# Two feed-forward passes: twelve of the 22 channel pairs made by seven 256-column block products each instead of eight, with the block adds on VectorE

## The chip, the core and the metric

The kernel runs on one core of one Trainium2 chip. A core has five engines that run their own instruction queues in order and meet at semaphores: TensorE (PE in the profile, with its weight loads as PEld), VectorE (DVE), ScalarE (ACT), GpSimd (POOL) and SyncE (SP), which here issues the DMAs. On-chip memory is SBUF, the matmuls write PSUM. The metric is the device time of one execution in microseconds; lower is better.

## The reference

The reference is a decoder trunk of two layers over 1024 positions of width 1024, float32. Each layer has a mixer and then a feed-forward pass, and each of the four sub-layers ends as x <- LayerNorm(alpha * x + f(x)). The change is in the feed-forward pass alone:

- up: u = x @ w_up, from 1024 to 5632 channels, in two halves of 2816;
- a causal depthwise convolution of width 3 over positions on all 5632 channels, plus a bias;
- gelu (tanh form) of the first half times the second half;
- down: from 2816 channels to 1024.

Products have to be of float32 accuracy.

## The kernel before, in words

**Tiles.** The 1024 positions are worked in two halves h of 512. A pass F(h, l) is the feed-forward pass of half h in layer l, so there are four: F00, F10, F01 and F11 (the program writes half and then layer). The input x of a pass lies transposed in SBUF, channels on partitions, as XTh and XTl: every float32 operand is split in a rounded part (h, sh, wh, ph) and a rest (l, sl, wl, pl), and `mm3` makes a product of three matmuls, h·l, l·h and h·h. A weight block of 128 by 1024 float32 (512 KB) comes by DMA into one of three `wraw` buffers; ACT copies it to `wh` in one instruction of 1024 columns, and POOL subtracts, two of 512 columns, to `wl` (`wload`).

**A pass.** `up(j)` makes channel pair j of 22: for each of two channel tiles, 8 blocks of K times three matmuls into one PSUM bank `pu` of 512 columns, so 48 matmuls of 128x512 a pair. Then the three taps of the convolution: one ACT instruction, two scalar_tensor_tensor (STT) on DVE, all of 512 columns; for h = 0 a copy of the last two columns for the other half (`halo`), for h = 1 two one-column ACT instructions with the correction `cor`. ACT makes the gelu of the first tile, POOL multiplies the two tiles, and ACT and POOL split the product into ph and pl. `down` takes the pairs in three groups (KG: 8, 8 and 6), in products of 512 columns into `pd` banks; DVE adds each bank to Z, the running sum of the sub-layer. F11 has its last group in `down_last`, which hands rows to the final norm.

**What sets the order.** The program text is written as generators, which `go(F, n)` runs for n steps and `mix(A, F, n)` interleaves; the scheduler under it then fixes an order for each engine. At the start of F00 the norm of the other half, `norm(1, g0)`, is mixed into its first steps; at the start of F11 the final norm of half 0 stands between its steps. PSUM has 2 banks for `pu`, 2 for the tag "c" and 4 for `pd`. The code around the change is printed here.

## Time and profile before

| what | value |
|---|---|
| median of 3 runs | 2339.61 us (2338.78 to 2342.55) |
| the profiled execution | 2340.53 us |
| its span, first to last instruction | 2338.8 us |
| PE busy | 2293.3 us, 98% |
| PEld, DVE, ACT, POOL busy | 82%, 50%, 43%, 60% |
| mean granted TensorE clock | 0.995 of full speed |
| F00's 22 pairs and their downs, about 568 to 910 us | PE busy 339.11 of 342.00 us |
| F11, about 1973 us to the end | PE busy 354.48 of 365.00 us |

The profiled execution is 1.7 us longer than its span, which lies outside the first and last instruction, and it is 0.9 us above the median of the runs. A busy PE is one whose pipeline holds some matmul; two of them overlap, so the time that a matmul costs is read from start to start, not from its duration.

### The profile page before, as it was taken

To read this page: it belongs to the slowest core of one execution; us is meant where nothing else is said; L and a number is where in the kernel's file an instruction comes from. 1 tells how busy PE (TensorE), PEld (TensorE's weight loads), DVE (VectorE), ACT (ScalarE), POOL (GpSimd) and SP (SyncE) were. 2 spreads that over 40 slices of the span, in tenths; PEclk is the share of its full clock that TensorE was granted. 3 is DMA by queue.
4 is the path that set the end of the run, shared out by engine and by line. 5 is a ranking of instruction groups with operands and counts; after the bars stand their busy time and mean duration, and the time that the engine had idled before them with its cause. 6 is when DMAs were issued, how large, how long until landed. Compare 5 with 4: busy or idle time off the path is not lost.

```text
span 2338.8 us, 30101 instructions
## 1 busy us (share of the span) xinstructions
PE 2293.3 (98%) x10959; PEld 1914.5 (82%) x10959; DVE 1176.0 (50%) x2176; ACT 1008.9 (43%) x1786; POOL 1391.8 (60%) x1313
## 2 busy tenths in 40 slices
PE   9999899999999999999999999999999999999998
PEld 7888789887888888788888887788888887888886
DVE  2532898746322223579972325589961446212214
ACT  4133998733433323434344552434243633534441
POOL 4442777556665656655566575655565666666672
PEclk9999999999999999999999999999999999999999
DMA  6153121352332333233323233223323233323340
GB/s 227 35 144 98 50 64 54 105 194 92 99 99 90 99 95 95 84 97 99 99 91 99 90 108 101 85 95 100 99 91 99 89 110 135 96 95 99 99 135 37
DMA packets 82988, 232.23 MB, mean 99 GB/s; under 512 B 10079, under 2 KB 24039, under 8 KB 82840
## 3 DMA queue, kind: packets, MB, share of 16 engines
q1 hardware_dynamic: 82840, 230.30, 31.2%
q8 instruction: 87, 1.43, 0.3%
q14 instruction: 61, 0.50, 0.1%
HBM read 213.44 MB, written 8.43 MB: 95 GB/s over the span
## 4 chain that ended last, share of the span: by engine, by line
PE 93%; DVE 3%; ACT 1%; issue 1%; POOL 1%; DMA 0%; SPq 0%; DVEq 0%; ACTq 0%
PE pu L77 13%; PE pu L79 13%; PE pu L78 13%; PE pd L77 9%; PE pd L78 9%; PE pd L79 9%; PE pt L563 2%; PE pca L79 1%; PE pcg L79 1%; PE pcg L77 1%; PE pca L77 1%; PE pcg L78 1%; PE pca L78 1%; PE O L571 1%; PE O L570 1%
## 5 line engine op out<-in xcount | busy, mean ns | idle before, releaser
L73 POOL TENSOR_TENSOR wl<-wraw,wh 128x512 fp32r<-128x512 f32 x680 | 889.1, 1330 | 704.7 <-ACT wh L70 693.7
L77 PE MATMUL pu<-XTl,wh 128*128 128x512 f32 x1440 | 564.7, 392 | 5.9 <-DVE acc L683 3.7
L79 PE MATMUL pu<-XTh,wh 128*128 128x512 f32 x1440 | 563.6, 391 | 0.0
L78 PE MATMUL pu<-XTh,wl 128*128 128x512 f32 x1440 | 563.0, 391 | 0.0
L70 ACT ACTIVATE wh<-wraw 128x1024 fp32r<-128x1024 f32 x340 | 359.6, 1058 | 414.3 <-PE pd L79 352.9
L682 DVE SCALAR_TENSOR_TENSOR acc<-pu,vec,acc 128x511 f32<-128x511 f32 x176 | 131.8, 749 | 513.0 <-ACT acc L680 264.6
L77 PEld LDWEIGHTS pu<-XTl,wh 128*128 128x128 f32 x1440 | 271.8, 189 | 62.8 <-issue 4.1
L758 DVE SCALAR_TENSOR_TENSOR cacc<-ht,vec,cacc 128x512 f32<-128x512 f32 x464 | 318.5, 751 | 5.5 <-ACT cacc L754 3.9
L678 ACT ACTIVATE acc<-pu,vec 128x510 f32<-128x510 f32 (+1 forms) x176 | 137.3, 780 | 424.0 <-PE pu L79 423.8
L79 PEld LDWEIGHTS pu<-XTh,wh 128*128 128x128 f32 x1440 | 271.5, 189 | 56.8
L78 PEld LDWEIGHTS pu<-XTh,wl 128*128 128x128 f32 x1440 | 271.7, 189 | 56.2
L77 PE MATMUL pd<-wl,ph 128*128 128x512 f32 x656 | 259.1, 396 | 0.0
L78 PE MATMUL pd<-wh,pl 128*128 128x512 f32 x656 | 258.8, 394 | 0.0
L79 PE MATMUL pd<-wh,ph 128*128 128x512 f32 x656 | 256.7, 395 | 0.0
L79 PEld LDWEIGHTS pd<-wh,ph 128*128 128x128 f32 x656 | 123.5, 188 | 29.0
L78 PEld LDWEIGHTS pd<-wh,pl 128*128 128x128 f32 x656 | 123.7, 189 | 28.6
L77 PEld LDWEIGHTS pd<-wl,ph 128*128 128x128 f32 x656 | 123.6, 188 | 28.4
L398 DVE TENSOR_TENSOR Z<-Z,pd 128x512 f32<-128x512 f32 x64 | 43.5, 683 | 180.1 <-PE pd L79 180.0
L683 DVE SCALAR_TENSOR_TENSOR acc<-pu,vec,acc 128x510 f32<-128x510 f32 x176 | 131.5, 747 | 4.7
L690 POOL TENSOR_TENSOR acc<-acc 128x512 f32<-128x512 f32 x88 | 113.7, 1292 | 25.0 <-DVE acc L683 17.6
L396 DVE SCALAR_TENSOR_TENSOR Z<-Z,pd 128x512 f32<-128x512 f32 x64 | 43.6, 682 | 156.6 <-PE pd L79 156.6
L540 POOL TENSOR_SCALAR P<-P,sm 128x64 f32<-128x64 f32 (+6 forms) x192 | 107.4, 583 | 21.9 <-DVE sm L534 12.8
(252 smaller groups left out, 3790.4 us busy)
## 6 DMA issues: line engine op xcount, KB each, us to landing
wraw<-wup SPq DMA_DIRECT2D x176, 512.0 KB, 3.5
wraw<-wdn SPq DMA_DIRECT2D x82, 512.0 KB, 3.5
wraw<-cwin SPq DMA_DIRECT2D x32, 512.0 KB, 3.5
wraw<-wout SPq DMA_DIRECT2D x16, 512.0 KB, 4.3
wraw<-cwout SPq DMA_DIRECT2D x16, 512.0 KB, 3.5
wraw<-wab SPq DMA_DIRECT2D x14, 512.0 KB, 3.9
gb<-lns SPq DMA_DIRECT2D x12, 512.0 KB, 4.2
B<-fd SPq DMA_DIRECT2D x8, 512.0 KB, 3.4
```

The lines of the kernel that those rows point to most:

```text
L70: nc.scalar.activation(wh[:, :n], raw[:, :n], AF.Copy)
L73: (leng or nc.gpsimd).tensor_tensor(wl[:, c], raw[:, c], wh[:, c].bitcast(F32), op=OP.subtract)
L77: nc.tensor.matmul(out_, ah, bl, start=first, stop=False)
L78: nc.tensor.matmul(out_, al, bh, start=False, stop=False)
L79: nc.tensor.matmul(out_, ah, bh, start=False, stop=last)
L540: nc.gpsimd.tensor_scalar(P[:, e, o:o + ln_], P[:, e, o:o + ln_], sm[:, e, i:i + 1], 0.0, op0=OP.mult, op1=OP.add)
L563: nc.tensor.transpose(pt[:, j, e * 128:(e + 1) * 128], P[:, e, o:o + kn], ident)
L678: nc.scalar.activation(a[:, 2 * h:], p[:, 2 * h:], AF.Identity, scale=cw[:, mt, 2:3], bias=col(cb, mt))
L682: nc.vector.scalar_tensor_tensor(a[:, 1:], p[:, :511], cw[:, mt, 1:2], a[:, 1:], op0=OP.mult, op1=OP.add)
L683: nc.vector.scalar_tensor_tensor(a[:, 2:], p[:, :510], cw[:, mt, 0:1], a[:, 2:], op0=OP.mult, op1=OP.add)
L690: nc.gpsimd.tensor_tensor(acc[0], acc[0], acc[1], op=OP.mult)
L758: nc.vector.scalar_tensor_tensor(c[0] if k else ht[:, :H], ht[:, k:k + H], dww[:, j, k:k + 1], c[0], op0=OP.mult, op1=OP.add)
```

## The change

It adds `QUICK = (4, 16)` and a flag `quick`, which F00 and F11 set. In such a pass the pairs 4 to 15 go through `up7` instead of `up`. `up7` sees the pair as a 2 by 2 by 2 block product (two channel tiles, two halves of K of 512, two halves of the positions of 256) and makes it of seven block products, in the Strassen-Winograd form. Each is 4 blocks of K times three matmuls of 128x256, so 84 matmuls of 256 columns a pair. That asks for:

- sums of weights: `prep(j)` makes s1 to s4 and the block w22' (the first operand of the last product) out of the two raw blocks `ra` and `rb` by 4 adds of 512 columns on DVE, and splits s1, s2 and s4 by ACT (sh) and DVE (sl); the four other blocks are split as before by ACT (wh) and POOL (wl);
- sums of x: `sums()`, run once a pass in six steps within the pairs 1 to 3, makes TA and TB, four sums with a split of each, on POOL, DVE and ACT;
- sums of products: a copy of 256 columns on ACT and 5 adds of 256 columns on DVE (`tt`, and back into PSUM `pa` and `pb`).

In all pairs of the two passes the product of the two halves and its rest `pl` move from POOL to DVE (`gated`). The downs of the first 16 pairs go in four groups of 4 pairs instead of two of 8, one unit of 24 matmuls beside each pair from 3 on, so a pass adds a bank to Z 32 times for the first 16 pairs where it was 16 times. TA and TB take the slots that the other half's XTh and XTl have, so `norm(1, g0)` comes after 32 steps of F00 instead of at its start, with its two rows of factors loaded again; in F11 one step instead of two goes beside each part of the final norm of half 0.

The diff, cut to its core (`taps3` is the old code of the taps, moved into a function; `mm3` gets a flag that changes no instruction):

```diff
+QUICK = (4, 16)
...
-    def ffn(h, l, tail=None):
+    def ffn(h, l, tail=None, quick=False):
...
+        def gated(j, acc):
+            eng = nc.vector if quick else nc.gpsimd
+            eng.tensor_tensor(acc[0], acc[0], acc[1], op=OP.mult)
+            hi = fp.tile([128, 512], F32R, name="ph", tag="p", bufs=18)
+            lo = fp.tile([128, 512], F32R, name="pl", tag="p", bufs=18)
+            split(hi, lo, acc[0], eng)
+            prod[j] = (hi, lo)
...
+        def sums():
+            ta, tb = A("xh", F32R, (128, 4, 4, 256), name="TA"), A("xl", F32R, (128, 4, 4, 256), name="TB")
+            X7["11"], X7["21"], X7["22"] = ((xh[:, a:a + 4, b:b + 256], xl[:, a:a + 4, b:b + 256])
+                                            for a, b in ((0, 0), (4, 0), (4, 256)))
+            X7["t1"], X7["t2"], X7["t3"], X7["t4"] = ((t_[:, i], t_[:, i + 1]) for t_ in (ta, tb) for i in (0, 2))
+            f = lambda a, b: (xh.bitcast(F32)[:, a:a + 2, b:b + 256], xl.bitcast(F32)[:, a:a + 2, b:b + 256])
+            for k in (0, 2):
+                u1, u2 = (fp.tile([128, 2, 2, 256], F32, name="ts", tag="nrm", bufs=2) for _ in range(2))
+                b11, b12, b22, b21 = u1[:, 0], u1[:, 1], u2[:, 0], u2[:, 1]
+                nc.gpsimd.tensor_tensor(b11, *f(k, 0), op=OP.add)
+                nc.vector.tensor_tensor(b12, *f(k, 256), op=OP.add)
+                nc.gpsimd.tensor_tensor(b21, *f(k + 4, 0), op=OP.add)
+                nc.vector.tensor_tensor(b22, *f(k + 4, 256), op=OP.add)
+                nc.vector.tensor_tensor(b22, b22, b12, op=OP.subtract)
+                nc.vector.tensor_tensor(b12, b12, b11, op=OP.subtract)
+                nc.vector.tensor_tensor(b11, b22, b11, op=OP.add)
+                nc.vector.tensor_tensor(b21, b21, b11, op=OP.subtract)
+                yield
+                for n, t_, e in (("t2", b11, nc.vector), ("t1", b12, nc.vector), ("t3", b22, nc.gpsimd),
+                                 ("t4", b21, nc.vector)):
+                    split(X7[n][0][:, k:k + 2], X7[n][1][:, k:k + 2], t_, e)
+                yield
...
+        def prep(j):
+            ra, rb = W4(F32, name="wraw"), W4(F32, name="wraw")
+            nc.sync.dma_start(ra, wup[l, 2 * j])
+            nc.sync.dma_start(rb, wup[l, 2 * j + 1])
+            s1, s2 = (fp.tile([128, 512], F32, name="ws", tag="ht", bufs=8) for _ in range(2))
+            a, b = slice(0, 512), slice(512, 1024)
+            add = lambda o, x_, y_, op: nc.vector.tensor_tensor(o, x_, y_, op=op)
+            w = {}
+
+            def pair(src):
+                h_, l_ = W4(F32R, name="wh", tag="wh"), W4(F32R, name="wl", tag="wl")
+                nc.scalar.activation(h_, src, AF.Copy)
+                for c in (a, b):
+                    nc.gpsimd.tensor_tensor(l_[:, c], src[:, c], h_[:, c].bitcast(F32), op=OP.subtract)
+                return [(h_[:, c], l_[:, c]) for c in (a, b)]
+
+            def one(src, eng):
+                h_, l_ = (fp.tile([128, 512], F32R, name=n, tag="ht", bufs=8) for n in ("sh", "sl"))
+                split(h_, l_, src, eng)
+                return h_, l_
+            add(s1, rb[:, a], rb[:, b], OP.add)
+            add(s2, s1, ra[:, a], OP.subtract)
+            w["11"], w["12"] = pair(ra)
+            w["s2"] = one(s2, nc.vector)
+            w["s1"] = one(s1, nc.vector)
+            yield w
+            add(rb[:, a], ra[:, a], rb[:, a], OP.subtract)
+            add(ra[:, b], ra[:, b], s2, OP.subtract)
+            w["s3"], w["22"] = pair(rb)
+            w["s4"] = one(ra[:, b], nc.vector)
+            yield
+
+
+        def prod7(o, w, x_, first=True):
+            for k in range(4):
+                s_ = slice(k * 128, (k + 1) * 128)
+                mm3(o, w[0][:, s_], w[1][:, s_], x_[0][:, k, :], x_[1][:, k, :], first and k == 0, k == 3, not first)
...
+        def up7(j):
+            w = W7.pop(j)
+            pa, pb = psn("u", "pa"), psn("c", "pb")
+            t_ = tmp("tt")
+            t_, v_ = t_[:, :256], t_[:, 256:]
+            c0, c1 = slice(0, 256), slice(256, 512)
+            add = lambda o, a, b: nc.vector.tensor_tensor(o, a, b, op=OP.add)
+            prod7(pa[:, c0], w["11"], X7["11"])
+            prod7(pb[:, c1], w["s2"], X7["t2"])
+            nc.scalar.activation(t_, pa[:, c0], AF.Copy)
+            add(t_, t_, pb[:, c1])
+            prod7(pa[:, c0], w["12"], X7["21"], False)
+            nxt = prep(j + 1) if j + 1 < QUICK[1] else None
+            prod7(pa[:, c1], w["s1"], X7["t1"])
+            add(v_, t_, pa[:, c1])
+            if nxt:
+                W7[j + 1] = next(nxt)
+            yield
+            prod7(pb[:, c0], w["s3"], X7["t3"])
+            add(pb[:, c1], v_, pb[:, c0])
+            prod7(pa[:, c1], w["s4"], X7["22"], False)
+            add(pa[:, c1], t_, pa[:, c1])
+            acc = [taps3(2 * j, pa)]
+            nc.scalar.activation(acc[0], acc[0], AF.Gelu_apprx_tanh)
+            prod7(pb[:, c0], w["22"], X7["t4"], False)
+            if nxt:
+                next(nxt)
+            add(pb[:, c0], t_, pb[:, c0])
+            acc.append(taps3(2 * j + 1, pb))
+            gated(j, acc)
+            yield
...
-            nc.gpsimd.tensor_tensor(acc[0], acc[0], acc[1], op=OP.mult)
-            hi = fp.tile([128, 512], F32R, name="ph", tag="p", bufs=18)
-            lo = fp.tile([128, 512], F32R, name="pl", tag="p", bufs=18)
-            split(hi, lo, acc[0], nc.gpsimd)
-            prod[j] = (hi, lo)
+            gated(j, acc)
...
+        if quick:
+
+            src = lambda a, dh, i: wdn[l, (a + 2 * i) // 8 * 8 + dh * 4 + (a // 2 + i) % 4]
+
+            def downs():
+                units = [(a, dh, i) for a in range(0, 16, 4) for dh in range(2) for i in range(2)]
+                w = wload(src(*units[0]))
+                yield
+                for n, (a, dh, i) in enumerate(units):
+                    if i == 0:
+                        p = [psn("d", "pd") for _ in range(4)]
+                        done = into(h, a == 0, False)
+                    for tt in range(4):
+                        ts = slice(tt * 128, (tt + 1) * 128)
+                        for k in range(2):
+                            (ah, al), s_ = prod[a + 2 * i + k], slice(k * 512, k * 512 + 512)
+                            mm3(p[tt], ah[:, ts], al[:, ts], w[0][:, s_], w[1][:, s_], i == k == 0, i == k == 1)
+                        if i:
+                            done(tt, dh, p[tt])
+                    if n + 1 < len(units):
+                        w = wload(src(*units[n + 1]))
+                    yield
+            dn, sm = downs(), sums()
+            last = down_last(tail) if tail else None
+            for j in range(NPAIR):
+                for i, _ in enumerate(up7(j) if QUICK[0] <= j < QUICK[1] else up(j)):
+                    if i == (j < 4) and j >= 3:
+                        next(dn, None)
+                    if QUICK[0] - 3 <= j < QUICK[0]:
+                        if next(sm, 1):
+                            lead7()
+                    if tail and 16 <= j < 19:
+                        next(last)
+                    yield
+            yield from last if tail else product(lambda k: prod[16 + k], lambda dh, i: src(16, dh, i), 6,
+                                                 into(h, False, True))
+            return
...
-    F00 = ffn(0, 0)
-    mix(norm(1, g0), F00, 1)
-    go(F00, 56)
+    F00 = ffn(0, 0, quick=True)
+    go(F00, 2 * QUICK[1])
+    g0 = affine(0)
+    mix(norm(1, g0), F00, 2)
+    go(F00, 4)
...
-    F11 = ffn(1, 1, final(1, g3))
+    F11 = ffn(1, 1, lambda tt: final(1, g3)(tt), quick=True)
     go(F01)
     for tt in range(4):
         final(0, g3)(tt)
-        go(F11, 2)
+        go(F11, 1)
+    go(F11, 2 * QUICK[1] - 4)
+    g3 = affine(3)
```

How the instructions of one pair stand, in the middle of F00. On **DVE** before, one whole pair of `up` (the first row is the first tap of the gelu tile):

```order
L682 SCALAR_TENSOR_TENSOR acc<-pu,vec,acc 128x511 [waits Activation_49,Pool_49]
L683 SCALAR_TENSOR_TENSOR acc<-pu,vec,acc 128x510 [waits DVE_49]
L685 COPY halo<-pu 128x2
L682 SCALAR_TENSOR_TENSOR acc<-pu,vec,acc 128x511 [waits Activation_49,Pool_49]
L683 SCALAR_TENSOR_TENSOR acc<-pu,vec,acc 128x510 [waits DVE_49]
L685 COPY halo<-pu 128x2
```

On DVE in the changed kernel, in a pair of F00 whose neighbouring unit of down ends a group of 4 (its four adds to Z stand here), from the add after the last product of one pair (`pb<-tt,pb`) on; `ws` and `wraw` are the sums of weights of a later pair, `sl` a rest of such a sum, `tt` the small sums of 256 columns:

```order
L772 TENSOR_TENSOR pb<-tt,pb 128x256 [waits PE_49]
L679 SCALAR_TENSOR_TENSOR acc<-pa,vec,acc 128x510 [waits DVE_49]
L681 COPY halo<-pa 128x2
L725 TENSOR_TENSOR ws<-wraw 128x512 [waits DMAHW7_49]
L678 SCALAR_TENSOR_TENSOR acc<-pb,vec,acc 128x511 [waits Activation_49]
L772 TENSOR_TENSOR tt<-tt,pb 128x256 [waits PE_49,Activation_49]
L400 TENSOR_TENSOR Z<-Z,pd 128x512 [waits PE_49]
L725 TENSOR_TENSOR ws<-ws,wraw 128x512 [waits DMAHW6_49,DVE_49]
L725 TENSOR_TENSOR wraw<-wraw 128x512 [waits DMAHW5_49,Pool_49]
L679 SCALAR_TENSOR_TENSOR acc<-pb,vec,acc 128x510 [waits DVE_49]
L681 COPY halo<-pb 128x2
L400 TENSOR_TENSOR Z<-Z,pd 128x512 [waits PE_49] x2
```

and right behind them, from the rest of s2 to the add onto `pb` (`acc<-acc` is the gated product, `pl` its rest, `tt<-tt,pa` the add of product s1):

```order
L64 TENSOR_TENSOR sl<-ws,sh 128x512 [waits Activation_49]
L686 TENSOR_TENSOR acc<-acc 128x512 [waits DVE_49]
L400 TENSOR_TENSOR Z<-Z,pd 128x512 [waits PE_49]
L772 TENSOR_TENSOR tt<-tt,pa 128x256 [waits PE_49]
L64 TENSOR_TENSOR pl<-acc,ph 128x512 [waits Activation_49]
L64 TENSOR_TENSOR sl<-ws,sh 128x512 [waits Activation_49]
L725 TENSOR_TENSOR wraw<-wraw,ws 128x512 [waits Pool_49]
L772 TENSOR_TENSOR pb<-tt,pb 128x256 [waits DVE_49,PE_49]
```

The two STT of a tile stood with nothing but a copy of two columns between them and the next tile's. Now sums of weights, their rests, the gated product and the adds to Z stand ahead of `tt<-tt,pa` and of the `pb<-tt,pb` at the end, on one in-order queue; in the pair beside it the Z rows are missing, and `pl` stands ahead of `tt<-tt,pa`.

On **PE** before, the end of one tile of `up` and the start of the next:

```order
L79 MATMUL pu<-XTh,wh 128x512
L77 MATMUL pu<-XTl,wh 128x512
L78 MATMUL pu<-XTh,wl 128x512
L79 MATMUL pu<-XTh,wh 128x512
L77 MATMUL pu<-XTl,wh 128x512 [waits DVE_49,Activation_49]
L78 MATMUL pu<-XTh,wl 128x512 [waits Pool_49]
L79 MATMUL pu<-XTh,wh 128x512
L77 MATMUL pu<-XTl,wh 128x512
```

On PE in the changed kernel, in a pair of the same kind, from the end of product s4 to the start of the last product (`pa<-XTh,wh`, `pb<-TA` are matmuls of the next pair that stand between them; the row with the wait starts the last product):

```order
L79 MATMUL pa<-XTl,sh 128x256
L80 MATMUL pa<-XTh,sl 128x256
L81 MATMUL pa<-XTh,sh 128x256
L80 MATMUL pa<-XTh,wl 128x256
L81 MATMUL pa<-XTh,wh 128x256
L81 MATMUL pb<-TA,sh 128x256
L79 MATMUL pb<-TA,sh 128x256
L80 MATMUL pb<-TA,sl 128x256
L81 MATMUL pb<-TA,sh 128x256
L79 MATMUL pb<-TA,sh 128x256
L79 MATMUL pb<-TB,wh 128x256 [waits DVE_49]
```

Each tile was a run of 24 matmuls that waited only for its weights and its bank; now the last product accumulates onto what DVE's `pb<-tt,pb` wrote, and waits for it.

## Rows read from the trace of the kernel before

**Rows 1.** The page's first lines and its chain that ended last.

```profile
PE 2293.3 (98%) x10959; PEld 1914.5 (82%) x10959; DVE 1176.0 (50%) x2176; ACT 1008.9 (43%) x1786; POOL 1391.8 (60%) x1313
...
PE 93%; DVE 3%; ACT 1%; issue 1%; POOL 1%; DMA 0%; SPq 0%; DVEq 0%; ACTq 0%
```

**Rows 2.** Windows, F00 and F11: length, busy time of each engine, PEclk, DMA share.

```profile
568.00:910.00 342.00, 339.11 (x1494) 278.75 (x1493) 100.09 (x176) 124.70 (x160) 214.31 (x168) 1.00 0.30 97
1973.00:2338.00 365.00, 354.48 (x1540) 289.97 (x1538) 103.38 (x146) 140.86 (x235) 220.66 (x169) 0.99 0.30 96
```

**Rows 3.** Timeline of PE, one tile of up: first matmul, and next tile's first.

```profile
759.87 0.39 PE L77 MATMUL pu<-XTl,wh 128*128 128x512 f32 x1
760.09 0.39 PE L78 MATMUL pu<-XTh,wl 128*128 128x512 f32 x1
...
765.31 0.39 PE L77 MATMUL pu<-XTl,wh 128*128 128x512 f32 x1
```

**Rows 4.** Timeline of PE, down: two rows that stand 21 matmuls apart.

```profile
706.54 0.40 PE L77 MATMUL pd<-wl,ph 128*128 128x512 f32 x1
...
711.42 0.40 PE L77 MATMUL pd<-wl,ph 128*128 128x512 f32 x1
```

**Rows 5.** Timelines of PE and of its weight loads, 256 columns, another stage.

```profile
72.39 0.28 PE L78 MATMUL pg<-wsh,vl 128*128 128x256 f32 x1
72.51 0.28 PE L79 MATMUL pg<-wsh,vh 128*128 128x256 f32 x1
...
73.10 0.28 PE L78 MATMUL pg<-wsh,vl 128*128 128x256 f32 x1
...
72.40 0.19 PEld L79 LDWEIGHTS pg<-wsh,vh 128*128 128x128 f32 x1
72.52 0.19 PEld L77 LDWEIGHTS pg<-wsl,vh 128*128 128x128 f32 x1
```

**Rows 6.** Groups by line and form: busy us, mean ns of one.

```profile
L682 DVE SCALAR_TENSOR_TENSOR acc<-pu,vec,acc 128x511 f32<-128x511 f32 x176 | 131.8, 749 | 513.0 <-ACT acc L680 264.6 <-ACT acc L678 247.6
L398 DVE TENSOR_TENSOR Z<-Z,pd 128x512 f32<-128x512 f32 x64 | 43.5, 683 | 180.1 <-PE pd L79 180.0
L685 DVE COPY halo<-pu 128x2 f32<-128x2 f32 x88 | 13.2, 150 | 0.0
L63 DVE TENSOR_TENSOR ptl<-pt,pth 128x256 fp32r<-128x256 f32 x24 | 9.9, 414 | 0.2
L678 ACT ACTIVATE acc<-pu,vec 128x512 f32<-128x512 f32 x88 | 68.7, 780 | 233.9 <-PE pu L79 233.7
L62 ACT ACTIVATE ph<-acc 128x512 fp32r<-128x512 f32 x88 | 55.0, 625 | 49.7 <-POOL acc L690 49.7
L690 POOL TENSOR_TENSOR acc<-acc 128x512 f32<-128x512 f32 x88 | 113.7, 1292 | 25.0 <-DVE acc L683 17.6 <-DVE halo L685 7.5
```

**Rows 7.** Instructions of tile mt (both inputs in SBUF) on DVE: min/median/max ns.

```profile
L63 DVE TENSOR_TENSOR mt<-mraw,mt x8: 677/693/1776, 497.3 to 509.2; 128x512 fp32r<-128x512 f32 x8
```

**Rows 8.** Timelines of DVE and POOL at the correction's adds of 44 columns.

```profile
906.40 1.32 DVE L663 TENSOR_TENSOR cor<-halo,vec 128x44 f32<-128x44 f32 x1
907.65 1.33 DVE L665 TENSOR_TENSOR cor<-halo,vec 128x44 f32<-128x44 f32 x1
908.90 0.20 DVE L664 TENSOR_TENSOR cor<-cor,cor 128x44 f32<-128x44 f32 x1
...
905.12 2.54 POOL L73 TENSOR_TENSOR wl<-wraw,wh 128x512 fp32r<-128x512 f32 x2 [1.65 <-ACT wh L70]
907.62 1.29 POOL L690 TENSOR_TENSOR acc<-acc 128x512 f32<-128x512 f32 x1
```

**Rows 9.** Timelines of DVE, POOL and PE where F00 meets the other half's norm.

```profile
575.45 2.11 DVE L624 SCALAR_TENSOR_TENSOR Z<-Z,mv,gb 128x1024 f32<-128x1024 f32 x1
577.49 2.28 DVE L625 SCALAR_TENSOR_TENSOR Z<-Z,tm,gb 128x1024 f32<-128x1024 f32 x1
...
575.20 3.49 POOL L73 TENSOR_TENSOR wl<-wraw,wh 128x512 fp32r<-128x512 f32 x2
...
577.31 0.39 PE L79 MATMUL pu<-XTh,wh 128*128 128x512 f32 x1
580.43 0.66 PE L636 MATMUL pn<-ident,Z 128*128 128x128 f32 x4 [2.73 <-DVE XTl L63]
```

**Rows 10.** DMA issues: count, KB each, us from issue to landing.

```profile
wraw<-wup SPq DMA_DIRECT2D x176, 512.0 KB, 3.5
```

More of the change, by code (lines that the diff above doesn't have):

```diff
@@ L74, in wload, with mm3 @@
         return wh, wl
-    def mm3(out_, ah, al, bh, bl, first, last):
-        nc.tensor.matmul(out_, ah, bl, start=first, stop=False)
-        nc.tensor.matmul(out_, al, bh, start=False, stop=False)
-        nc.tensor.matmul(out_, ah, bh, start=False, stop=last)
+    def mm3(out_, ah, al, bh, bl, first, last, more=False):
+        nc.tensor.matmul(out_, ah, bl, start=first, stop=False, skip_group_check=more)
+        nc.tensor.matmul(out_, al, bh, start=False, stop=False, skip_group_check=more)
+        nc.tensor.matmul(out_, ah, bh, start=False, stop=last, skip_group_check=more)
     def mtile(out_, w, xh, xl, kn=8):
@@ L668, in ffn, with taps3 @@
         prod = {}
+        def taps3(mt, p):
+            a = tmp("acc")
+            nc.scalar.activation(a[:, 2 * h:], p[:, 2 * h:], AF.Identity, scale=cw[:, mt, 2:3], bias=col(cb, mt))
+            for i in range(2 * h):
+                nc.scalar.activation(a[:, i:i + 1], p[:, i:i + 1], AF.Identity, scale=cw[:, mt, 2:3],
+                                     bias=cor[:, mt, i:i + 1])
+            nc.vector.scalar_tensor_tensor(a[:, 1:], p[:, :511], cw[:, mt, 1:2], a[:, 1:], op0=OP.mult, op1=OP.add)
+            nc.vector.scalar_tensor_tensor(a[:, 2:], p[:, :510], cw[:, mt, 0:1], a[:, 2:], op0=OP.mult, op1=OP.add)
+            if h == 0:
+                nc.vector.tensor_copy(hal[:, mt, :], p[:, 510:512])
+            return a
@@ new lines, in gated @@
+        def gated(j, acc):
[5 more added lines that the diff above has]
+            prod[j] = (hi, lo)
+        X7 = {}
+        def sums():
[20 more added lines that the diff above has]
+                yield
@@ new lines, in prod7, with lead7 @@
+        def prod7(o, w, x_, first=True):
+            for k in range(4):
+                s_ = slice(k * 128, (k + 1) * 128)
+                mm3(o, w[0][:, s_], w[1][:, s_], x_[0][:, k, :], x_[1][:, k, :], first and k == 0, k == 3, not first)
+        W7 = {}
+        def lead7():
+            if QUICK[0] not in W7:
+                W7[-1] = prep(QUICK[0])
+                W7[QUICK[0]] = next(W7[-1])
+            else:
+                next(W7.pop(-1), None)
+        def up7(j):
[29 more added lines that the diff above has]
+            yield
@@ L676, in up @@
                 mtile(p, w, xh, xl)
-                a = tmp("acc")
-                nc.scalar.activation(a[:, 2 * h:], p[:, 2 * h:], AF.Identity, scale=cw[:, mt, 2:3], bias=col(cb, mt))
-                for i in range(2 * h):
-                    nc.scalar.activation(a[:, i:i + 1], p[:, i:i + 1], AF.Identity, scale=cw[:, mt, 2:3],
-                                         bias=cor[:, mt, i:i + 1])
-                nc.vector.scalar_tensor_tensor(a[:, 1:], p[:, :511], cw[:, mt, 1:2], a[:, 1:], op0=OP.mult, op1=OP.add)
-                nc.vector.scalar_tensor_tensor(a[:, 2:], p[:, :510], cw[:, mt, 0:1], a[:, 2:], op0=OP.mult, op1=OP.add)
-                if h == 0:
-                    nc.vector.tensor_copy(hal[:, mt, :], p[:, 510:512])
-                acc.append(a)
+                acc.append(taps3(mt, p))
                 if e == 0:
-                    nc.scalar.activation(a, a, AF.Gelu_apprx_tanh)
+                    nc.scalar.activation(acc[0], acc[0], AF.Gelu_apprx_tanh)
                     yield
-            nc.gpsimd.tensor_tensor(acc[0], acc[0], acc[1], op=OP.mult)
-            hi = fp.tile([128, 512], F32R, name="ph", tag="p", bufs=18)
-            lo = fp.tile([128, 512], F32R, name="pl", tag="p", bufs=18)
-            split(hi, lo, acc[0], nc.gpsimd)
-            prod[j] = (hi, lo)
+            gated(j, acc)
             yield
```

## The prediction

> **What bounds the kernel now.** The page's first lines say that TensorE is busy for 98% of the span, and the chain that ended last lies on PE for 93% of its length [rows 1]. So I read PE by its start-to-start times, and then the stretches of the two passes that change. The windows show that F00 leaves PE idle for 342.00 - 339.11 = 2.9 us, while DVE works for 100 us of 342, ACT for 125 and POOL for 214 [rows 2]. F11 leaves 10.5 us, most of it at the start and in the tail. Before, the two passes are matmul work at the full clock with hardly a gap: the time can only fall if PE has fewer columns to do, and it rises if any other engine that PE waits for gets slower than PE.
>
> **PE's side.** In up, 24 matmuls of 512 columns take 765.31 - 759.87 = 5.44 us, 0.2267 each, or 10.88 us a pair [rows 3]. A matmul of 256 columns starts 0.118 us behind the one before it (six intervals from 72.39 to 73.10), each with its own weight load of 0.19 us beside it [rows 5]. A quick pair is then 84 x 0.118 = 9.91 us, which saves 0.97. Over 24 pairs this is 23.2 us. A unit of down beside each pair is 24 x 4.88 / 21 = 5.58 us [rows 4]. So pair and unit take 16.46 us before, and 15.49 if PE never waits.
>
> The Trainium skill, "TensorE: Matmul & The Clock Gate", section "Wait — 56ns, not 53.3ns?", gives a start-to-start of N / 2.4 GHz plus some 2.5 ns. That would be 215.8 and 109.2 ns, 10.36 and 9.17 us a pair, and an estimated saving of 28.5 us. The rows here are 227 and 118 ns, so the measured ones stand in the sum.
>
> **DVE's side.** Per quick pair DVE did 4 STT of 0.749 us and two small copies. It gets 4 adds of weights, 3 rests sl, the gated product and its rest: nine instructions of 512 columns whose inputs both lie in SBUF. It gets 5 adds of 256 columns, and every second pair has 4 adds to Z. From rows: 0.69 for one of the nine when nothing disturbs it [rows 7]; 0.41 for 256 columns, 0.68 for Z and 0.15 for the copy of two columns [rows 6].
>
> Now I walk the queue in the order that stands in the section on the change. Call B the pair with the adds to Z, A the one beside it. From the end of a pair's last product, PE has seven matmuls of the next pair left in one case and two in the other (0.83 or 0.24 us), then the unit of down (5.58), then 24 matmuls (2.83) up to the end of product s1: 9.24 us ahead of B's s1, 8.65 ahead of A's. In that time DVE does, ahead of `tt<-tt,pa`: A two adds of 256, three STT, two copies and six of the nine, 0.82 + 2.25 + 0.30 + 4.14 = 7.51 us; B the same with four Z adds (2.72) and without pl (0.69), 9.54 us. Behind s1, the last product may start once `pb<-tt,pb` is done. A: 0.41 + 2 x 0.69 + 0.41 = 2.20 us, B with pl 2.89. PE has other products for 4.85 us there in A, 5.44 in B. Undisturbed, A has 2.65 us to spare and B 5.44 - 0.30 - 2.89 = 2.25. PE would stay the bound.
>
> **What the nine instructions meet.** They are not undisturbed. The trace has few DVE instructions with both inputs in SBUF that meet POOL, but these speak clearly. The split of mt took 0.69 us in the median and 1.776 at most [rows 7], 1.08 more. Adds of only 44 columns took 1.32 and 1.33 us while POOL ran its 1.29 us subtracts back to back, and 0.20 when it paused [rows 8]: 1.12 more each. Norm steps of Z took 2.11 and 2.28 us, and the two POOL subtracts beside them 3.49 [rows 9] instead of 2.54 [rows 8]. So such a DVE instruction waits until POOL's running one has ended, and POOL then waits for DVE. STT on PSUM (one input in SBUF) kept its 0.749 [rows 6].
>
> The Trainium skill says this too: "SBUF — State Buffer", section "Who interferes with whom", has an exclusive lock on a port pair that DVE's second SBUF input shares with GpSimd. It speaks against this change, and the trace agrees, with 1.32 us for 44 columns.
>
> POOL loses the gated product and its rest and keeps six subtracts of 1.292 us a pair, 7.75 of some 16.2 us: 48% of the time. If an instruction of the nine arrives at any moment, it meets one with that chance. What it then waits is 1.1 us by the rows above if POOL has just begun, up to 1.25 if it loses its turn. So 0.53 to 0.60 us each; I take 0.565, since the subtracts come in pairs and a hold by the first leaves the next instruction to the second. The bounds are 0.31 (48% of the mean rest of an instruction, 0.65) and 0.8 (three quarters of them at 1.1, when the queues fall into step).
>
> With a hold of 0.565 each: B arrives at `tt<-tt,pa` 9.54 + 5 x 0.565 - 9.24 = 3.13 us late, and needs 2.89 + 3 x 0.565 = 4.59 more, 7.72 against 5.44: PE waits 2.3 us. A: 7.51 + 6 x 0.565 - 8.65 = 2.25, and 2.20 + 1.13 = 3.33 more, 5.58 against 4.85: PE waits 0.7. The mean is 1.5 us a pair, so pair and unit take 15.49 + 1.5 = 16.99 us, 0.53 more than before, and 24 of them 12.8 us.
>
> Bounds by the same steps: with 0.31, B waits 0.2 and A nothing, a mean of 0.1, 15.6 us, and 24 x -0.86 = -20.6 us. With 0.8, B waits 4.15 and A 2.6, a mean of 3.4, 18.89 us, +58 us. With 0.5, B waits 1.75 and A 0.2, and the pair takes what it took before: the time turns on this one number.
>
> **The rest.** F00 loses the stop of 2.73 us where the norm's split kept the transposes waiting [rows 9]; the same norm goes later, beside quick pairs or after them, so I count -2.7 and, for what it meets there, the sums of x (18 more DVE instructions of 512 in three pairs of each pass, 12.4 us beside pairs in which DVE has two thirds of its time free) and F11's extra one-column instructions on ACT, +3 together, between 0 and 16. The adds of weights wait for DMAs that land 3.5 us after issue [rows 10]; the buffer that `rb` takes comes free with the rest of s4 on DVE, 2.89 + 0.69 = 3.6 us behind a pair's s1, so its data lie there 7.1 us behind s1, and the first add of weights stands some 8 us behind it: a split that is held by 1 us makes that add late too. This is in the upper bound. ACT gets three copies of 0.625 and one of 256 columns more a pair, some 12 x 2.3 = 28 us on 125 of 342 [rows 2, 6]: it stays below half.
>
> **Sum**, against the profiled execution of 2340.5 us (1.7 outside its span; 0.9 above the median of 2339.6): 2340.5 + 12.8 - 2.7 + 3 = 2353.6, for a median 0.9 lower: 2353 us.
>
> **The rivals.** A measurement of this kernel tells some 0.2% (4.7 us) from no change.
>
> First, DVE and POOL interleave well, and PE stays the bound: 2340.5 - 23.2 - 2.7 = 2315 without any hold, 2329 with a hold of 0.4 (B waits 0.95, A nothing, 24 x -0.5). For it: undisturbed, each pair has over 2 us to spare, and POOL has lost 2.6 us a pair. Against it: four of POOL's six subtracts follow from the ACT copies that start when the unit of down ends, and so lie right around s1, where the queue is tightest. It decides in favour of faster if a hold is below 0.46 us. Chance 0.27.
>
> Second, gain and loss cancel: a hold of 0.46 to 0.53, 2336 to 2345. Chance 0.12.
>
> Third, my forecast and its upper part, DVE's queue held by POOL: 2345 to 2400. Chance 0.58.
>
> Fourth, weight loads or the queue of PE do not keep up with 84 short matmuls. At 0.19 us a load and nothing hidden, a pair would be 15.9 us and the time 140 us more. The rows of pg, where loads of 0.19 start 0.118 apart [rows 5], speak against it. Chance 0.03, with whatever else makes it slower still.
>
> So faster 0.27, same 0.12, slower 0.61. The range goes from 2320 to 2398.
>
> **What would show it.** Right: in the quick pairs the matmuls of the last product (`pb<-TB,wh`) sit idle some 1 to 3 us behind DVE's `pb<-tt,pb`, more in pairs with adds to Z; the mean of `sl`, `pl`, `ws` and `wraw` on DVE is well above 0.69, about 1.2; POOL's subtracts are above 1.5; PE's busy share in F00 falls below 95%. PE's matmuls of 256 columns start 0.118 apart within a product. Wrong: those means stay near 0.8 and PE waits nowhere (first rival), matmuls of 256 start further apart (fourth), or PE waits for weights, that is for POOL's `wl`, ACT's `wh` or a DMA, which would put the cause on ACT's queue or the three `wraw` buffers instead of DVE's.

## The result and the profile after

The changed kernel takes 2373.93 us in the median of 4 runs (2373.54 to 2374.21), beside 2340.49 us for the kernel before: 1.0141 times as long, 95% interval 1.0129 to 1.0154. That is 33.4 us slower, where 12.5 were forecast (2353 against 2340.5; 13.1 by the terms of the sum, which start from 2339.6, the median of the first three runs before) with a range up to 2398. The direction was right, the size was not.

The page's first lines and the chain that ended last, after:

```profile
PE 2283.5 (96%) x11823; PEld 1941.0 (82%) x11823; DVE 1504.1 (63%) x2620; ACT 1065.6 (45%) x1898; POOL 1337.6 (56%) x1237
...
PE 76%; DVE 13%; DMA 4%; issue 3%; ACT 3%; POOL 1%; SPq 0%; DVEq 0%; ACTq 0%; POOLq 0%
```

Against [rows 1], PE's share of the chain falls from 93% to 76% and DVE's rises from 3% to 13%. PE now waits for DVE.

Where the time went is read from the first and last matmul of the convolution's products `pca`, which the change doesn't touch, and the span's end (2338.8 and 2372.3 us). Instructions of tile pca, before and then after (count, min/median/max ns, first and last start us):

```profile
L77 PE MATMUL pca<-XTl,wh x128: 389/389/389, 998.1 to 1594.5; 128*128 128x512 f32 x128
```

```profile
L79 PE MATMUL pca<-XTl,wh x128: 389/389/389, 1017.1 to 1611.6; 128*128 128x512 f32 x128
```

Up to the first convolution, with F00 in it, +19.0 us; between the two, -1.9 (594.5 against 596.4); behind the last, with F11 in it, +16.4 (760.7 against 744.3).

In a window within F00's quick pairs, after (length, PE, PEld, DVE, ACT, POOL busy, PEclk, DMA share, GB/s); its 984 matmuls are some nine pairs of 84, each with its unit of down of 24:

```profile
655.00:816.00 161.00, 145.71 (x984) 132.20 (x983) 132.38 (x199) 69.64 (x101) 81.33 (x56) 1.00 0.26 89
```

PE is idle for 15.3 us of 161 there, at a granted clock of 1.00, the 2.4 GHz level. The waits of PE, after (us in total, times, longest): in this stretch, in F11's quick pairs (2040 to 2230), at F00's start (560 to 610) and at F11's (1973 to 2040):

```profile
PE pb L79 <- DVE pb L772: 9.0, 9, 1.3
PE pa L79 <- DVE tt L772: 4.8, 7, 0.8
PE pb L80 <- DVE sl L64: 1.4, 2, 0.8
...
PE pb L79 <- DVE pb L772: 12.9, 10, 1.4
PE pa L79 <- DVE tt L772: 1.4, 2, 0.8
...
PE pu L79 <- DVE halo L681: 7.9, 2, 4.0
PE pu L79 <- DVE mv L620: 1.8, 1, 1.8
...
PE pu L79 <- DVE acc L679: 8.0, 3, 3.7
PE pb L80 <- DVE sl L64: 2.7, 1, 2.7
```

Before, F11's start (1973 to 2040):

```profile
PE pu L77 <- DVE acc L683: 3.7, 1, 3.7
```

Two things are to be seen. The quick pairs idle for 15.2 + 14.3 = 29.5 us in the two windows, mostly where the prediction said, at the last product behind `pb<-tt,pb`. And in the four pairs ahead of them, which are ordinary, PE idles for 9.7 and 8.0 us, since a `pu` bank comes free late: its taps stand on DVE behind something else. F11's first quick pair then waits 2.7 us for its first `sl`. Before, F00's start had one wait of 2.73 us, for the norm's split [rows 9], and F11's start one of 3.7 us for a `pu` bank.

DVE and POOL in the same window of F00, after, groups by line (busy us, mean ns of one, idle before it):

```profile
L64 DVE TENSOR_TENSOR sl<-ws,sh 128x512 fp32r<-128x512 f32 x18 | 22.3, 1238 | 1.5 <-ACT sh L63 1.0
L686 DVE TENSOR_TENSOR acc<-acc 128x512 f32<-128x512 f32 x9 | 14.9, 1654 | 0.0
L725 DVE TENSOR_TENSOR wraw<-wraw,ws 128x512 f32<-128x512 f32 x10 | 13.3, 1334 | 0.8 <-POOL wl L732 0.8
L725 DVE TENSOR_TENSOR ws<-wraw 128x512 f32<-128x512 f32 x9 | 8.9, 989 | 11.6 <-DMA wraw<-wup 11.5
L64 DVE TENSOR_TENSOR pl<-acc,ph 128x512 fp32r<-128x512 f32 x9 | 8.1, 896 | 2.8 <-ACT ph L63 2.8
L64 DVE TENSOR_TENSOR sl<-wraw,sh 128x512 fp32r<-128x512 f32 x10 | 7.4, 742 | 4.5 <-ACT sh L63 4.5
L725 DVE TENSOR_TENSOR ws<-ws,wraw 128x512 f32<-128x512 f32 x9 | 6.6, 730 | 0.0
L725 DVE TENSOR_TENSOR wraw<-wraw 128x512 f32<-128x512 f32 x9 | 6.2, 683 | 0.0
L772 DVE TENSOR_TENSOR pb<-tt,pb 128x256 f32<-128x256 f32 x18 | 7.5, 418 | 0.0
...
L732 POOL TENSOR_TENSOR wl<-wraw,wh 128x512 fp32r<-128x512 f32 x36 | 51.2, 1443 | 74.8 <-ACT wh L730 74.8
L74 POOL TENSOR_TENSOR wl<-wraw,wh 128x512 fp32r<-128x512 f32 x19 | 30.8, 1642 | 2.1 <-ACT wh L71 2.1
```

The first eight rows are the nine instructions of a pair: 87.7 us for 83, 1.06 each, against 0.69 undisturbed [rows 7]. The hold is 0.37 us on average and unevenly spread. Of the 82 that start in this window, the 36 that overlap no POOL instruction take 0.69 us, the 46 that overlap one take 1.33. So the gated product takes 1.65, the add `wraw<-wraw` 0.68. Adds with one input in PSUM keep their 0.42. POOL's subtracts take 1.44 for the quick pairs and 1.64 for the downs, instead of 1.33 on average before. DVE also sits idle for 11.5 us, 1.3 a pair, until raw weights land.

In F11 (2040 to 2230) the nine take 0.94 on average, but the one that stands right ahead of `pb<-tt,pb` takes 1.08 more than undisturbed:

```profile
L725 DVE TENSOR_TENSOR wraw<-wraw,ws 128x512 f32<-128x512 f32 x11 | 19.5, 1773 | 0.0
```

The matmuls themselves are as forecast. Timeline of PE, after, around one stop:

```profile
724.24 0.28 PE L80 MATMUL pb<-TA,sl 128*128 128x256 f32 x1
724.36 0.28 PE L81 MATMUL pb<-TA,sh 128*128 128x256 f32 x1
724.47 0.28 PE L79 MATMUL pb<-TA,sh 128*128 128x256 f32 x1
725.66 0.39 PE L79 MATMUL pb<-TB,wh 128*128 128x256 f32 x1 [0.92 <-DVE pb L772]
725.88 0.28 PE L80 MATMUL pb<-TB,wl 128*128 128x256 f32 x1
```

They start 0.118 us apart. An idle of 0.92 us costs 725.66 - 724.47 - 0.12 = 1.07 us from start to start, since matmuls overlap. Summed so over all starts more than 0.35 us apart, the stops are 18.1 us in F00's twelve quick pairs and 16.3 in F11's (without its first `sl`), 1.43 a pair. Behind a stop the next matmul comes 0.22 us later (725.88) instead of 0.118; these and the shorter stops add 4.9 us, 0.21 a pair.

What DVE does when the ordinary pairs stop PE, after, timelines of PE and DVE at the start of F00:

```profile
576.33 0.39 PE L81 MATMUL pu<-XTh,wh 128*128 128x512 f32 x1
580.66 0.47 PE L79 MATMUL pu<-XTl,wh 128*128 128x512 f32 x1 [3.95 <-DVE halo L681]
...
576.15 1.65 DVE L711 TENSOR_TENSOR ts<-ts 128x512 f32<-128x512 f32 x1
577.73 0.68 DVE L64 TENSOR_TENSOR TA<-ts,TA 128x512 fp32r<-128x512 f32 x1
578.33 0.68 DVE L712 TENSOR_TENSOR ts<-ts 128x512 f32<-128x512 f32 x1
578.93 0.74 DVE L678 SCALAR_TENSOR_TENSOR acc<-pu,vec,acc 128x511 f32<-128x511 f32 x1
...
585.85 3.10 DVE L626 SCALAR_TENSOR_TENSOR Z<-Z,mv,gb 128x1024 f32<-128x1024 f32 x2 [1.94 <-DMA gb<-lns]
588.87 0.74 DVE L679 SCALAR_TENSOR_TENSOR acc<-pu,vec,acc 128x510 f32<-128x510 f32 x1
...
589.71 3.46 DVE L627 SCALAR_TENSOR_TENSOR Z<-Z,tm,gb 128x1024 f32<-128x1024 f32 x2
```

The taps (`acc<-pu`) stand behind the sums of x (`ts`, `TA`), some of which take 1.65 us for 0.68 of work. Then they stand behind the norm of the other half: its text comes after 32 steps, but its steps on Z run at 586 to 602 us in the scheduler's order, and its first one waits 1.94 us for the reloaded factors while the tap L679 is queued behind it.

### The profile page after: what moved, and what is told of

It is laid out like the page before. It is cut to its first block, busy times and chain, and to the rows that moved or that the text cites. A ratio compares the mean times of both kernels' runs of the same rounds, so it can differ in the third digit from the quotient of the medians.

```text
span 2372.3 us, 32434 instructions
## 1 busy us (share of the span) xinstructions
PE 2283.5 (96%) x11823; PEld 1941.0 (82%) x11823; DVE 1504.1 (63%) x2620; ACT 1065.6 (45%) x1898; POOL 1337.6 (56%) x1237
## 4 chain that ended last, share of the span: by engine, by line
PE 76%; DVE 13%; DMA 4%; issue 3%; ACT 3%; POOL 1%; SPq 0%; DVEq 0%; ACTq 0%; POOLq 0%
PE pu L79 9%; PE pu L80 9%; PE pu L81 9%; PE pd L79 8%; PE pd L81 8%; PE pd L80 8%; DMA wraw<-wup 3%; DVE wraw L725 2%; PE pt L565 2%; DVE sl L64 1%; PE pcg L79 1%; PE pca L79 1%; PE pcg L81 1%; PE pca L81 1%; PE pca L80 1%
## 5 line engine op out<-in xcount | busy, mean ns | idle before, releaser
L74 POOL TENSOR_TENSOR wl<-wraw,wh 128x512 fp32r<-128x512 f32 x584 | 792.0, 1378 | 588.1 <-ACT wh L71 587.3
L71 ACT ACTIVATE wh<-wraw 128x1024 fp32r<-128x1024 f32 x292 | 308.4, 1057 | 289.0 <-PE pd L81 240.5
L79 PE MATMUL pu<-XTl,wh 128*128 128x512 f32 x1056 | 416.8, 395 | 19.5 <-DVE acc L679 8.0
L81 PE MATMUL pu<-XTh,wh 128*128 128x512 f32 x1056 | 414.7, 393 | 0.0
L80 PE MATMUL pu<-XTh,wl 128*128 128x512 f32 x1056 | 414.2, 392 | 0.0
L79 PEld LDWEIGHTS pu<-XTl,wh 128*128 128x128 f32 x1056 | 200.3, 190 | 63.4 <-issue 9.8
L732 POOL TENSOR_TENSOR wl<-wraw,wh 128x512 fp32r<-128x512 f32 x96 | 137.3, 1451 | 193.0 <-ACT wh L730 188.9
L81 PEld LDWEIGHTS pu<-XTh,wh 128*128 128x128 f32 x1056 | 199.8, 189 | 42.0
L80 PEld LDWEIGHTS pu<-XTh,wl 128*128 128x128 f32 x1056 | 200.3, 190 | 41.0
L64 DVE TENSOR_TENSOR ptl<-pt,pth 128x512 fp32r<-128x512 f32 (+1 forms) x160 | 101.0, 645 | 28.2 <-ACT pth L63 22.7
L508 ACT ACTIVATE P<-P,mx 128x64 f32<-128x64 f32 (+6 forms) x192 | 114.8, 607 | 5.1 <-DVE mx L500 4.0
```

The source lines that it names most:

```text
L64: (leng or nc.vector).tensor_tensor(lo, src, hi.bitcast(F32), op=OP.subtract)
L71: nc.scalar.activation(wh[:, :n], raw[:, :n], AF.Copy)
L74: (leng or nc.gpsimd).tensor_tensor(wl[:, c], raw[:, c], wh[:, c].bitcast(F32), op=OP.subtract)
L79: nc.tensor.matmul(out_, ah, bl, start=first, stop=False, skip_group_check=more)
L80: nc.tensor.matmul(out_, al, bh, start=False, stop=False, skip_group_check=more)
L81: nc.tensor.matmul(out_, ah, bh, start=False, stop=last, skip_group_check=more)
```

## Experiments

All times are medians, each with the kernel before on the same chip (2340.1 to 2341.3 us); ratios are to that kernel, with their interval.

**Moves alone.** Every pair goes through `up`, and no sums are made:

```diff
-                for i, _ in enumerate(up7(j) if QUICK[0] <= j < QUICK[1] else up(j)):
+                for i, _ in enumerate(up(j)):
...
-                    if QUICK[0] - 3 <= j < QUICK[0]:
-                        if next(sm, 1):
-                            lead7()
```

> All 22 pairs of both passes through up, 48 matmuls of 512 columns, and no sums of x; the gated product on VectorE, downs in groups of four pairs, the later norm and the reloaded factors stay. My theory (the 22 us that the forecast lacked come from the sums of x that stand in VectorE's queue ahead of the taps in pairs 1 to 3): the stops of TensorE in pairs 0 to 3 go, 2336 to 2345 us. Rival (they come from the norm's new place and its reloaded factors): the stops stay, 2352 to 2365 us.

2340.5 us, 0.9997 (0.9987 to 1.0006), within the theory's band. The gated product on VectorE, the downs in groups of four pairs with their added sums into Z, and the norm's new place cost nothing that can be measured.

**Moves and sums.** The same, but `next(sm, 1)` stays, so the sums are made and not used. (`sums` has four steps, which fall into pairs 1 and 2; the other two of the six steps in pairs 1 to 3 are `lead7`, the first `prep`, and this kernel doesn't have it.)

> As e1_moves, with the sums of x made in pairs 1 to 3 but used by no product. My theory: the stops of 2 to 4 us in pairs 0 to 3 are back in both passes, 12 to 22 us above e1_moves, 2350 to 2362 us. Rival (norm and factors): within 4 us of e1_moves.

2353.83 us, 1.0056 (1.0041 to 1.0071): 13.3 us above the run without sums (9.4 between the spans of the two profiled executions, 2350.2 and 2340.8). PE's waits at F00's start are back (560 to 610 us, this kernel), and F11's start has 8.0 us of them where the run without sums has 3.7:

```profile
PE pu L79 <- DVE halo L681: 7.0, 2, 3.9
PE pu L79 <- DVE mv L620: 1.1, 1, 1.1
```

The first theory holds. The norm at the same place costs nothing without the sums.

**Sums without GpSimd's reads.** The kernel with the moves and sums, with memsets for the subtracts of the weights of the pairs 0 to 3 in both passes (the rests of these weights are left out):

```diff
-                w = wload(wup[l, mt])
+                w = wload(wup[l, mt], blank=quick and j < 4)
...
+            if blank:
+                nc.gpsimd.memset(wl[:, c].bitcast(F32), 0.0)
+            else:
```

> As e2_moves_sums, with memsets instead of GpSimd's subtracts for the weights of the pairs 0 to 3 of the two passes: the rests of these weights are left out, GpSimd reads nothing there. Theory (the sums of x stop TensorE because GpSimd holds VectorE's instructions in them): back to 2340 to 2345 us. Rival (18 instructions and the norm's in one in-order run ahead of the taps are enough by themselves): 2350 to 2355 us.

2337.74 us, 0.9988 (0.9979 to 0.9997), 2.3 below the theory's band: all of the 13.3 us are gone, and some 3 more. DVE has the same instructions in the same run ahead of the taps, so their number alone isn't the cause; what differs is that POOL reads nothing for the weights there. The memsets free more than the sums: the norm's first steps on Z fall from 1.50 to 1.28 us, and F11's start has 1.9 us of waits left, fewer than before the change. How much of the 13.3 us is the hold on the sums alone isn't separated. Timeline of DVE, this kernel, the same place as above:

```profile
572.43 1.67 DVE L714 TENSOR_TENSOR ts<-ts 128x512 f32<-128x512 f32 x1
574.02 0.68 DVE L64 TENSOR_TENSOR TA<-ts,TA 128x512 fp32r<-128x512 f32 x1
574.63 0.68 DVE L715 TENSOR_TENSOR ts<-ts 128x512 f32<-128x512 f32 x1
575.23 0.74 DVE L681 SCALAR_TENSOR_TENSOR acc<-pu,vec,acc 128x511 f32<-128x511 f32 x1
```

The one at 572.43 still meets a POOL instruction of the sums themselves. The tap comes 3.7 us earlier than after the change, 2.8 earlier than in the run with moves and sums (578.03), and PE's waits at F00's start fall to 2.7 us.

**Quick pairs without GpSimd's reads.** The changed kernel with such memsets in `prep` and in the first four groups of down (the rests of these weights are left out):

```diff
-                    nc.gpsimd.tensor_tensor(l_[:, c], src[:, c], h_[:, c].bitcast(F32), op=OP.subtract)
+                    nc.gpsimd.memset(l_[:, c].bitcast(F32), 0.0)
...
-                    w = wload(src(*units[n + 1]))
+                    w = wload(src(*units[n + 1]), blank=True)
```

> The changed kernel, in which GpSimd's subtracts for the weights of the quick pairs and of the first four down groups are memsets of the same tile: the rests of these weights are left out, and GpSimd reads nothing there. VectorE keeps its nine instructions with two SBUF inputs. My theory (they are held by GpSimd's subtracts, not slow by themselves): they take 0.69 us each, TensorE waits under 0.5 us a quick pair instead of 1.4, 2340 to 2352 us. Rival (VectorE has simply too much to do in its order): 2362 to 2376 us.

2332.55 us, 0.9963 (0.9949 to 0.9977), 41.4 us below the changed kernel and 8.7 below the one before, 7.5 below the theory's band. Groups on DVE in the same window of F00, and the window, this kernel:

```profile
L64 DVE TENSOR_TENSOR sl<-ws,sh 128x512 fp32r<-128x512 f32 x18 | 12.3, 685 | 0.0
L689 DVE TENSOR_TENSOR acc<-acc 128x512 f32<-128x512 f32 x11 | 7.6, 690 | 0.2
L728 DVE TENSOR_TENSOR ws<-wraw 128x512 f32<-128x512 f32 x9 | 6.2, 692 | 10.7 <-DMA wraw<-wup 10.7
...
655.00:816.00 161.00, 161.00 (x1111) 149.36 (x1111) 115.26 (x223) 78.94 (x113) 32.56 (x63) 1.00 0.32 104
```

The same instructions take 0.69 us, PE is busy for all of the 161 us, and works through 1111 matmuls instead of 984. Of the nine, 32 overlap a memset there and take 0.69 all the same: it is GpSimd's reads that hold them, not its being busy. DVE still waits 10.7 us for raw weights, 1.2 a pair, as after the change (1.3): so that wait costs nothing here while DVE has time to spare, and isn't the cause by itself. The stops at the starts stay (9.8 us of waits in F00, 7.1 in F11), as the subtracts for pairs 0 to 3 do.

**One input instead of two** (the sums of weights, the rests and the product of the halves are left out):

```diff
-            add = lambda o, x_, y_, op: nc.vector.tensor_tensor(o, x_, y_, op=op)
+            add = lambda o, x_, y_, op: nc.vector.tensor_scalar(o, x_, 0.5, None, op0=OP.mult)
...
-                split(h_, l_, src, eng)
+                nc.scalar.activation(h_, src, AF.Copy)
+                eng.tensor_scalar(l_, h_.bitcast(F32), 0.001, None, op0=OP.mult)
```

> The changed kernel, in which the nine instructions of a quick pair (adds of weights, rests, gated product and its rest) read one SBUF input by tensor_scalar instead of two: the sums, rests and the product of the two halves are left out, the instructions and their waits on other engines stay. My theory (VectorE's queue is held by GpSimd in these nine): they take 0.55 to 0.65 us each instead of 0.9 to 1.5, TensorE waits less than 0.4 us a quick pair instead of 1.43, 2338 to 2350 us. Rival (the raw weights land too late, and VectorE waits for them at the first add of weights): within 8 us of 2374 us.

2337.11 us, 0.9987 (0.9978 to 0.9997), just below the stated band. The nine take 0.60 us on average, as the theory said, and PE has no stop in F00's quick pairs, but 5.0 us of waits in F11's. But this run is a weaker proof than the one before it: the instructions also got shorter, and some were held all the same. Groups on DVE, 655 to 816 us, this kernel:

```profile
L732 DVE TENSOR_SCALAR wraw<-wraw 128x512 f32<-128x512 f32 x18 | 17.2, 957 | 5.3 <-POOL wl L739 5.3
L732 DVE TENSOR_SCALAR ws<-ws 128x512 f32<-128x512 f32 x9 | 3.7, 411 | 0.0
```

**The gated product back on GpSimd:**

```diff
-            eng = nc.vector if quick else nc.gpsimd
+            eng = nc.gpsimd
```

> The changed kernel with the gated product and its rest back on GpSimd. My theory: VectorE has two held instructions less a pair, GpSimd is busy 64% of a pair, so each of the other seven waits some 0.75 us; by the walk of the prediction TensorE waits 0.4 us a quick pair instead of 1.4, and the DVE queue of pairs 0 to 3 is shorter too: 2342 to 2360 us. Rival (weights that land late): 2368 to 2378 us.

2361.28 us, 1.0088 (1.0073 to 1.0103), 12.7 below the changed kernel and 1 us above my band. PE idles for 2.6 us in the window of F00's quick pairs instead of 15.2, but F11 gains nothing (14.3 us of waits, as after the change). There PE waits for ACT's `wh` and POOL's `wl` too (2045 to 2225 us, this kernel):

```profile
PE pb L79 <- DVE pb L772: 4.0, 5, 0.9
PE pa L79 <- DVE tt L772: 3.4, 3, 1.2
PE pa L79 <- ACT wh L730: 2.3, 2, 1.3
PE pb L80 <- DVE sl L64: 2.2, 2, 1.2
PE pa L80 <- POOL wl L732: 1.4, 2, 1.0
```

**Rests of weights on VectorE.** All four subtracts of `prep` there, the gated product on GpSimd; or two of the four, the gated product on VectorE:

```diff
-                    nc.gpsimd.tensor_tensor(l_[:, c], src[:, c], h_[:, c].bitcast(F32), op=OP.subtract)
+                    nc.vector.tensor_tensor(l_[:, c], src[:, c], h_[:, c].bitcast(F32), op=OP.subtract)
...
-            w["11"], w["12"] = pair(ra)
+            w["11"], w["12"] = pair(ra, nc.gpsimd)
...
-            w["s3"], w["22"] = pair(rb)
+            w["s3"], w["22"] = pair(rb, nc.vector)
```

> The changed kernel with all four subtracts for the weights of a quick pair on VectorE (0.6 us each there, 1.29 on GpSimd), and the gated product and its rest back on GpSimd: eleven instructions with two SBUF inputs a pair on VectorE, four on GpSimd. My theory (VectorE and GpSimd take turns, so what counts is the sum of both, 11 x 0.6 + 4 x 1.25 = 11.6 us a pair against 12.9 in the changed kernel): a smaller hold than the 0.36 us measured there, TensorE waits some 0.7 us less a quick pair, 2350 to 2364 us. Rival (VectorE's own work decides, 13.2 against 12 us a pair): TensorE waits as much or more, 2372 to 2390 us.

> The changed kernel with two of the four subtracts (those of rb's blocks) on VectorE, the gated product staying there too: again eleven and four. My theory: 2350 to 2366 us, near e9_rests_vector, since the sum is the same. Rival: 2372 to 2390 us.

2377.19 us, 1.0156 (1.0141 to 1.0171), and 2366.35 us, 1.0111 (1.0094 to 1.0128). The first lies in its rival's band, the second 0.35 us above its theory's. Of two kernels with the same sum over both engines, one is 3 us slower than the changed kernel and one 8 us faster: the sum doesn't decide. In the first, PE waits for ACT's copy `tt` (4.6 us of the window) and for `tt<-tt,pb` (3.1), other places than the forecast's: moved work is late elsewhere in the queues.

**F00 alone quick,** gated product on GpSimd, F11 as before the change:

> F00 quick with the gated product on GpSimd, F11 as before the change. In e4_gated_pool the stretch from F00's start to the first convolution took 433.0 us against 432.3 before, so 2338 to 2344 us if the loss of that kernel sits in F11 alone; 2346 to 2356 us if F11's order gave time back elsewhere.

2340.53 us, 0.9998 (0.9989 to 1.0007), within the first band. What F00's quick pairs give, its start takes.

**Sums spread.** The same with the sums in six steps over pairs 0 to 2, and the first `prep` in pair 3:

```diff
                 nc.vector.tensor_tensor(b22, b22, b12, op=OP.subtract)
+                yield
                 nc.vector.tensor_tensor(b12, b12, b11, op=OP.subtract)
...
-                    if QUICK[0] - 3 <= j < QUICK[0]:
+                    if QUICK[0] - 4 <= j < QUICK[0]:
```

> As e6_f00_only, the same sums of x in six steps over pairs 0 to 3, three VectorE instructions in a step instead of six and three over pairs 1 to 3. My theory (the taps stand behind the run of six): the stops of 4.3, 1.2, 3.3 and 1.5 us at the start of F00 fall to 4 us in all, 2331 to 2337 us. Rival (VectorE's work of sums and norm together is what stops TensorE, in whatever steps): 2338 to 2344 us.

2339.24 us, 0.9993 (0.9984 to 1.0002): the rival's band. The stops stay (4.33, 1.25 and 3.34 us from start to start).

**Later start.** F00 alone, quick pairs 6 to 15, the sums in eight steps over pairs 1 to 4, and the first `prep` in pair 5:

> As e6_f00_only, ten quick pairs (6 to 15) and the sums in eight steps over pairs 1 to 5. The sums meet less of the norm: the stops at the start of F00 fall to 2 us in all, -8, and two quick pairs less cost 1 us: 2331 to 2338 us. Rival (the norm alone stops TensorE there): 2339 to 2345 us.

2352.94 us, 1.0051 (1.0038 to 1.0063): worse than both said. The stops at the start stay (4.34, 1.38 and 3.34), and the quick pairs now wait for POOL's `wl` and ACT's `wh` as well (2.5 and 2.0 us between 650 and 820). Why another first pair brings the scheduler to that order stays open.

**Late norm.** The kernel with spread sums, the norm's factors loaded into four tiles of the weights' pool, so that they come free only after the quick pairs, and its steps on Z cut into halves of 512 columns:

```diff
-    g0 = affine(0)
+    g0 = affine2(0)
...
+                t_ = fp.tile([128, 512], F32, name="gh", tag="ht", bufs=8)
```

> As e7_sums_spread (F00 alone quick, gated product on GpSimd, sums spread), with the factors of the norm of the other half loaded into four tiles that come free only after the quick pairs, so that its steps on VectorE can't stand among the sums in pairs 0 to 3. Theory (sums and norm together stop TensorE there): the stops of 4.3, 1.25 and 3.3 us shrink to 3 us in all, and the norm costs 1 to 3 us later: 2331 to 2336 us. Rival (the sums alone suffice): 2338 to 2343 us.

2340.47 us, 1.0005 (0.9996 to 1.0013), the rival's band. The second and third stop at F00's start are gone, the first stays (PE waits 3.9 us for a `halo`), and the norm's steps at the end of the quick pairs stop PE for 3.9 us in turn: moved, not won. No version here beats the kernel before beyond its interval, save the three that leave work out (2332.55, 2337.11 and 2337.74 us).

## Why the prediction was wrong in size

**PE's side was right.** Matmuls of 256 columns start 0.118 us apart, and a quick pair without any hold runs at that pace: with GpSimd's reads gone, PE was busy for the whole window. The fourth rival (weight loads, PE's queue) is out.

**The cost of the quick pairs came out near, for reasons only half right.** Forecast: PE waits 1.5 us a pair, +0.53, 12.8 us in all. Measured: stops of 1.43 a pair and 0.21 for the starts behind them, less 0.97 saved, 0.67 or 16.1 us in all. The run without GpSimd's reads says 41.4 - 23.2 = 18.2, what it gives back less the saving. The place was right, too, and so was the cause: without POOL's reads the waits vanish, and DVE's own work fits. (The POOL work in [rows 8] is two subtracts and a gated product, not subtracts alone; nothing hangs on it.) But the hold was 0.37 us an instruction in F00 and 0.25 in F11, not 0.565, and nearer to the lower bound of 0.31. By the walk, 0.37 would make PE wait 0.36 us a pair. The walk spread the hold evenly, but in F11 it falls on the add right ahead of `pb<-tt,pb`. And the walk had DVE never idle, but it waits 1.3 us a pair for raw weights and some more for ACT's copies; I had left the weights to the upper bound. This idle costs nothing without the hold; that it uses up the slack with it is argued, and no run shows it alone. Two errors all but cancelled, which is luck.

**The step that failed is "The rest", which counted the sums of x and the norm's new place at +3 together, between 0 and 16.** With the -2.7 it made +0.3 us, and at its bound 16 - 2.7 = 13.3. It measured 33.4 - 16.1 = 17.3 by the trace, or 33.4 - 18.2 = 15.2 by the run without GpSimd's reads, beyond its bound either way. Of these, 13.3 (by chance the same number) are the sums beside ordinary pairs (the run with moves and sums less the one without). I had reasoned that DVE has two thirds of its time free there. That is the average over F00 [rows 2]. At its start (560 to 610 us) DVE was busy for 32.3 of 50 us already before the change, with the norm, and for 47.3 after it. There the sums stand in a run ahead of the taps, some of them held by POOL, and PE has only two `pu` banks, so it stops once a tile's taps are later than the next tile's 5.44 us [rows 3] cover. The hold was weighed for the quick pairs and left out for the 18 instructions next to them, where POOL reads SBUF too, for the weights and for the sums. They also stand in two pairs, not three. I also read the norm's new place off the text (beside quick pairs or after them) instead of off the order, in which its steps stand among the sums at 586 to 602 us. The experiment without the subtracts shows that GpSimd's reads are the cause, as it took all 13.3 us back; it freed the norm's steps together with the sums.

Counted over every start of the two traces beyond 0.227 or 0.118 us, the stops at the starts of F00 and F11 are 22.2 us, before 6.8. Of the 15.4 more, 2.9 are F11's first quick pair, whose `prep` stands in the pairs ahead as well. Matmuls that start late behind these stops add 2.6. With the 16.1 of the quick pairs this makes 34.1; the other stretches are 0.5 us shorter, and the two spans are 33.5 apart. Why the starts stop somewhat longer than with the sums alone isn't settled.

**The rivals.** The third, the forecast's own, happened. The first (PE stays the bound) said 2315 us without any hold; with the quick pairs freed of it the time was 2332.55, since the stops at the starts stayed. Neither that nor the second happened. Of the signs, PE was busy for 90.5% of the window, under the 95% named, and the nine's mean was 1.06, not 1.2; POOL's subtracts lie on both sides of the 1.5 named. The forecast's sign came from the right mechanism.
